# Converted weights of a hybrid decoder step held as half-unit tiles instead of whole-unit tiles

## The chip, the cores and the metric

The kernel runs on one core of a Trainium2 chip. The metric is the device time of one execution in microseconds (us); the time of a kernel is the median of several runs. A measurement is compared with runs of the kernel before on the same chip.

## The reference

The reference is one inference step of a decoder trunk with two layers, for a prompt of 512 tokens and eight samples of four new tokens, 544 columns in all, with 1024 features:

```
h = x
layer 0:  h += SSD(rmsnorm(h))     # in: 1024 -> 5120 + 32, convolution of width 4, scan, gate, norm, out: 2048 -> 1024
          h += MLP(rmsnorm(h))     # square(relu(u @ w_up)) @ w_down, 1024 -> 4096 -> 1024
layer 1:  h += HGRN2(rmsnorm(h))   # in: 1024 -> 4 x 1024, recurrence, gate, norm, out: 1024 -> 1024
          h += MLP(rmsnorm(h))
y = rmsnorm(h)
```

It returns y for both parts and the new states of convolution, SSD and HGRN2. Everything is float32.

## The kernel before, in words

**Products of two parts.** A float32 matrix is not multiplied as it is. Each weight and each operand is split into a high part (a cast to float32r, `hi`) and a low part (`lo = raw - hi`), and a product is the sum of three: hi times high, hi times low, lo times high. `split` (L187) does it with one cast on ScalarE (L188) and one subtraction on VectorE (L189).

**Units.** Weights arrive as units of 128 x 1024 float32, half a megabyte: eight blocks of 128 x 128. For an input or MLP unit the blocks are the eight k of one output tile; for an output unit (`out_unit`, and the end of `hgrn`) they are four k times two output tiles, so that block `k * 256 + i * 128` belongs to k and output tile i, and both halves of the unit hold two k of both tiles. There are 56 units of the SSD layer, 64 of each MLP and 40 of HGRN2.

**From DRAM to TensorE.** `load_next` (L166) loads a unit into one of three raw tiles over SyncE's queue; a load waits until the raw tile it overwrites has been read for the last time. `conv_unit` (L191) issues the loads that are due and then converts one unit: a cast into a tile `whi` and a subtraction into a tile `wlo`, each 128 x 1024, each tag with two buffers (pool `wcv`, L104). So a cast waits until the last matmul that read `whi` of the unit two back is done, and a subtraction likewise for `wlo`. The first two units are converted in two pieces of 512 columns into the same tiles. In the SSD layer every third unit from 6 on is "added" (L221): its low part is made ahead by `added_low` (L224), a negated cast on ScalarE into a tile of its own and two accumulating DMAs from GpSimd's queue, so that `conv_unit` has only the cast left (L206). `take` (L252) is called when a unit is needed and converts up to one unit ahead.

**TensorE's order.** `products` (L298) issues, for one unit and one output tile, three products per k in two column halves of 272: 48 matmuls for eight k. In the SSD layer (`"w" in sp`) they go in groups of four k: first hi with both operand parts for the four, then lo. Elsewhere k by k. The results stand in `acc`, two PSUM tiles of two banks each (`psb`).

**The MLP** computes a quarter of its columns directly and the rest by a scheme of seven products on 2 x 2 blocks (`seventh`, `form`); these take tiles `fh` and `fl` of 128 x 512 with five buffers of their own. In the last three quarters the first two down units are cut (L79): d0 k 0 to 3, the last products of the scheme, d0 k 4 and 5, d1 k 0 to 5, d0 k 6 and 7, d1 k 6 and 7, then the other units. The last two down units of the kernel go to `finish` (L1362), which multiplies and norms column half by column half.

**What sets the order of work.** The program is traced in Python. Beside the units, generators run as background: `scan`, `gated_norm`, `levels`, `states` and others give up control with a number of ticks, and `products` ticks after every six pairs of matmuls. The framework then orders each engine's instructions by priority and by a model of when they are ready, hands out buffers, and sets semaphores. Loads (L196) and, outside the MLPs, conversions (L201) have high priority from unit 3 on. On the chip each engine works through its own list in order, and an instruction that has to wait holds up those behind it. SyncE's list holds weight loads (L171), the decay rows of the scan read back from DRAM (`rows`, L558, tile `w`), states (L620, L741) and the convolution's output (L470).

In the SSD layer, ScalarE and VectorE do, beside the conversions: `conv_tile` (L466 to L483: copies `pre` out of PSUM, the convolution `cacc`, `th`, then `xs` or `BC`), the decay weights (L568 to L571 `E` and `w`, L623), the scan (`xd`, `xt`, `hT`, `y`), the gates (L505 `thz`, L506 `zs`) and the gated norm (L763 on; its split of `yh` and `yl` at L772 and after).

Of the kernel before, what the change touches and what calls it, by code (L numbers as in the profile page):

```python
# [16 lines left out]
P = 128  # L17
# [79 lines left out]
def trunk(ctx: ExitStack, tc: tile.TileContext, io):  # L97
# [93 lines left out]
    def conv_unit():  # L191
        if state["conv"] >= len(jobs):
            return
        (kind, u), at = jobs[state["conv"]]
        state["conv"] += 1
        with tc.high_priority() if u > 2 else ExitStack():  # L196
            while state["load"] <= min(at + (3 if mp else 2 if "w" in sp else 1), len(loads) - 1):
                if loads[state["load"]][0] != "u" and not mp:
                    break
                load_next()  # L200
        with tc.high_priority() if u > 2 and not mp else ExitStack():  # L201
            if kind == "u":
# [12 lines left out]
            else:  # L215
                hi, lo = form(kind, u)
        ready[kind, u] = (hi, lo)

    lows = {}

    def added(u):  # L221
        return 3 < u < U_MLP and u % 3 == 0

    def added_low(u):  # L224

        raw = loaded["u", u]
        lows[u] = sp["w"].tile([P, 1024], F32R, tag="wlo", bufs=1, name=f"wlo{u}")
        nc.scalar.activation(lows[u], raw, AF.Copy, scale=-1.0)
        for c in (0, 512):
            nc.gpsimd.dma_start(lows[u][:, c : c + 512], io["W"][u][:, c : c + 512], accum_op=ADD)  # L230

    def form(name, u):

        a1 = loaded["u", u]
        v = loaded.get(("v", u))
        if name == "n6":
            s2 = mp["w"].tile([P, 512], F32, tag="s2", bufs=2, name=f"s2_{u}")
            nc.vector.tensor_tensor(s2, v[:, :512], a1[:, :512], ADD)
# [11 lines left out]
        return hi, lo  # L250

    def take(key):  # L252
        i = place[key]
# [11 lines left out]
    def unit(u):  # L265
        return take(("u", u))
# [28 lines left out]
            while any(e[2] == name for e in q):  # L295
                step(q)

    def products(ps, hi, lo, ops, first, last):  # L298

        n = len(ops)  # L300
        order = [(k, j) for k in range(n) for j in range(3)]
        if "w" in sp:

            order = [(k, j) for k0 in range(0, n, 4) for js in ((0, 1), (2,)) for k in range(k0, min(k0 + 4, n)) for j in js]
        for i, (k, j) in enumerate(order):
            oh, ol = ops[k]
            w, o = ((hi, oh), (hi, ol), (lo, oh))[j]
            for h in range(2):
                nc.tensor.matmul(  # L309
                    ps[:, h, :HF], w[:, k, :], o[:, h * HF : (h + 1) * HF],  # L310
                    start=(first and i == 0), stop=(last and i == len(order) - 1),
                )
            if i % 6 == 5:
                tick()
# [88 lines left out]
    def ssd(then):  # L403
# [51 lines left out]

        def conv_tile(u, ct, dst, rep):

            hi, lo = unit(u)
            ps = acc_tile(f"ps{u}")
            products(  # L460
                ps, hi.rearrange("p (k m) -> p k m", m=P), lo.rearrange("p (k m) -> p k m", m=P), uops, True, True
            )
# [31 lines left out]
            return pool.tile([P, T], F32, tag="zs", bufs=4, name=f"zs{u}")  # L494

        def z_product(u, ops=uops):
            hi, lo = unit(u)
            ps = acc_tile(f"ps{u}")
            products(ps, hi.rearrange("p (k m) -> p k m", m=P), lo.rearrange("p (k m) -> p k m", m=P), ops, True, True)
            return ps  # L500

        def silu2(u, zs, z):
# [5 lines left out]
        def first_gates():  # L508

            nonlocal rb  # L510
            zs = [zs_tile(u) for u in range(4)]
            w = [[t.rearrange("p (k m) -> p k m", m=P) for t in unit(u)] for u in range(2)]
            ps = [acc_tile(f"ps{u}") for u in range(2)]
            for k in range(KT):
                for i in range(2):
                    products(ps[i], w[i][0][:, k : k + 1], w[i][1][:, k : k + 1], xops[k : k + 1], k == 0, k == KT - 1)
            for i in range(2):
                nc.scalar.copy(v3(zs[i]), ps[i][:, :, :HF])
            res = []
# [399 lines left out]
    def mlp(name, plan, v0, then, last=False):  # L919
# [47 lines left out]
                yield 2.6  # L967

        background(operands(), name, wait=3)
        m8 = lambda w: w.rearrange("p (k m) -> p k m", m=P)  # L970

        def up(u):
            ps = acc_tile(f"pm{u}")
            products(ps, *map(m8, unit(u)), uops, True, True)
            return ps

        def g_tiles(u, a):
# [14 lines left out]
        def seventh(name_, u):  # L992
# [8 lines left out]
            hi, lo = map(m8, take((name_, u)))  # L1001
            for k in range(4):
                oh, ol = fops[name_, k]
                for j, (w, o) in enumerate(((hi, oh), (hi, ol), (lo, oh))):
                    nc.tensor.matmul(  # L1005
                        ps, w[:, k, :], o, start=(name_ in ("p1", "p2", "q7") and k == 0 and j == 0),
                        stop=(k == 3 and j == 2), skip_group_check=name_ in ("n6", "n5", "p3", "q4"),
                    )
            tick()
# [26 lines left out]
        for x_ in plan:  # L1036
# [9 lines left out]
            elif x_[0] == "d":  # L1046
                _, u, k0, k1, m, q = x_
                if k0 == 0:
# [4 lines left out]
                    if last and q == MLP_GROUPS - 1 and m >= KT - 2:  # L1053
# [6 lines left out]
                    acc[m][1] = [m8(w) for w in unit(u)]  # L1060
                ps, (hi, lo) = acc[m]
# [12 lines left out]
    def hgrn(then):  # L1074
# [37 lines left out]
        background(rstd_steps(1.0 / D, "hn", res, nt, wait=3), "hn", wait=3)  # L1112

        def product(u):
            hi, lo = unit(u)
            ps = acc_tile(f"ps{u}")
            products(ps, hi.rearrange("p (k m) -> p k m", m=P), lo.rearrange("p (k m) -> p k m", m=P), uops, True, True)
            return ps

        def project(u, name, ps=None):  # L1120
# [224 lines left out]
        for half in range(2):  # L1345
            if half:
                drain("hs7")
            for mp in range(4):
                hi, lo = unit(u)
                u += 1  # L1350
                for i in range(2):
                    ps = acc_tile(f"pho{half}_{mp}_{i}")
                    products(
                        ps, hi.rearrange("p (k m) -> p k m", k=4)[:, :, i * P : (i + 1) * P],
                        lo.rearrange("p (k m) -> p k m", k=4)[:, :, i * P : (i + 1) * P], ops[4 * half : 4 * half + 4], True, True,
                    )
                    add_to_x(2 * mp + i, ps, then if half == 1 else None)
        es.close()

# [2 lines left out]
    def finish(w, ops, pss):  # L1362

        es = ExitStack()
        pool = es.enter_context(tc.tile_pool(name="f_pool", bufs=2, reuse_waits="tile"))
        ws = [[t.rearrange("p (k m) -> p k m", m=P) for t in hl] for hl in w]
        ms2 = (KT - 2, KT - 1)
        for h in range(2):
            hs = slice(h * HF, (h + 1) * HF)
            sqs = []  # L1370
            for m, (hi, lo), ps in zip(ms2, ws, pss):
                for k, (oh, ol) in enumerate(ops):
                    for j, (a, o) in enumerate(((hi, oh), (hi, ol), (lo, oh))):
                        nc.tensor.matmul(
                            ps[:, h, :HF], a[:, k, :], o[:, hs], start=(k == 0 and j == 0), stop=(k == len(ops) - 1 and j == 2)
                        )
                sq = pool.tile([P, HF], F32, tag=f"sq{m}", name=f"sq{m}_{h}")
                nc.vector.tensor_tensor(x[m][:, hs], ps[:, h, :HF], x[m][:, hs], ADD)
# [171 lines left out]
```

## Time and profile before

| | |
|---|---|
| time before, median of 3 runs | 1575.24 us (1573.57 to 1576.04) |
| the profiled execution: its own time | 1573.53 us |
| the profiled execution: its span | 1571.7 us |
| mean granted clock of TensorE | 0.991 |
| casts of whole or half units, L188 / L206 | 161 / 17 |
| subtractions of units, L189 | 161 |

The span runs from the first to the last instruction that the profile shows; the time around it is 1.8 us in that execution. In the profile PE is TensorE's matmuls, PEld its weight loads, DVE VectorE, ACT ScalarE, POOL GpSimd, SP SyncE; a q behind the name means the engine's sequencer. A row names line, engine, operation, and output <- inputs by the program's names without buffer numbers; L188 and L189 are lines of a helper, so that only the tile's name tells whose conversion it is. Starts are in us from the span's start. A tile's low part made by `added_low` is also called `wlo`.

### The profile page before, as it was taken

What the parts mean: (1) busy time and instruction counts of PE and PEld (TensorE: products, weight loads), DVE (VectorE), ACT (ScalarE), POOL (GpSimd) and SP (SyncE); (2) the same over time, 40 slices, a digit from 0 to 9 for tenths busy, and PEclk for the clock granted to TensorE, in tenths of its full rate; (3) what the DMA queues carried; (4) which work ended last, traced back from release to release, by engine and by line L of the source; (5) the groups of instructions that cost most, each with busy time, mean ns of one, the idle gap of its engine ahead of it and who ended that gap; (6) DMA issues with size and microseconds to landing.
All of it is one profiled execution on the core that took longest, in us unless ns stands there. A gap on an engine that the chain in (4) does not pass through costs nothing.

```text
span 1571.7 us, 32262 instructions
## 1 busy us (share of the span) xinstructions
PE 1539.2 (98%) x13420; PEld 1477.0 (94%) x13420; DVE 1081.3 (69%) x1985; ACT 741.6 (47%) x1332; POOL 122.4 (8%) x195
## 2 busy tenths in 40 slices
PE   8999899999999999999999999999999999999997
PEld 7998789898999999999999999999999999999996
DVE  7878698968877555474655788888877655474544
ACT  5666675665344436273553332333344446263552
POOL 3112011110001001010000000000001001010001
PEclk9999899999999999999999999999999999999998
DMA  6545547574436245463323232323226245463311
GB/s 197 154 129 138 150 107 227 121 220 123 129 103 181 86 121 135 121 166 81 116 63 108 69 99 84 105 89 110 70 96 175 81 128 128 121 166 93 105 55 57
DMA packets 86337, 188.90 MB, mean 120 GB/s; under 512 B 12784, under 2 KB 33168, under 8 KB 86192
## 3 DMA queue, kind: packets, MB, share of 16 engines
q1 hardware_dynamic: 73120, 164.21, 33.3%
q0 software_dynamic: 11808, 21.50, 8.5%
q8 instruction: 105, 1.72, 0.5%
q10 hardware_dynamic: 1264, 1.14, 0.2%
q14 instruction: 40, 0.33, 0.1%
HBM read 169.64 MB, written 17.18 MB: 119 GB/s over the span
## 4 chain that ended last, share of the span: by engine, by line
PE 90%; DVE 3%; ACT 3%; DMA 2%; issue 1%; POOL 0%; POOLq 0%; SPq 0%; ACTq 0%; DVEq 0%
PE ps L309 25%; PE pd L309 23%; PE pp L1005 11%; PE pm L309 6%; PE po L309 6%; PE pc L1005 5%; PE pho L309 3%; DMA w<-cum_d 1%; DVE wlo L189 1%; PE pa L1144 1%; ACT whi L188 1%; PE py L602 1%; ACT w L570 1%; PE pS L1247 1%; PE po L1270 1%
## 5 line engine op out<-in xcount | busy, mean ns | idle before, releaser
L188 ACT CAST whi<-raw 128x1024 fp32r<-128x1024 f32 (+1 forms) x161 | 167.1, 1038 | 337.6 <-PE ps L309 110.5
L189 DVE TENSOR_TENSOR wlo<-raw,whi 128x1024 fp32r<-128x1024 f32 (+1 forms) x161 | 195.6, 1215 | 35.3 <-ACT whi L188 30.1
L309 PE MATMUL pd<-gh,wlo 128*128 128x272 f32 x992 | 205.8, 289 | 0.8
L309 PE MATMUL pd<-gh,whi 128*128 128x272 f32 x992 | 205.8, 288 | 0.0
L309 PE MATMUL pd<-gl,whi 128*128 128x272 f32 x992 | 205.3, 288 | 0.0
L309 PEld LDWEIGHTS pd<-gh,wlo 128*128 128x128 f32 x992 | 155.6, 188 | 2.1 <-DVE wlo L189 2.1
L309 PEld LDWEIGHTS pd<-gh,whi 128*128 128x128 f32 x992 | 156.0, 188 | 0.0
L309 PEld LDWEIGHTS pd<-gl,whi 128*128 128x128 f32 x992 | 155.5, 188 | 0.0
L309 PE MATMUL ps<-uh_s,whi 128*128 128x272 f32 x576 | 125.0, 298 | 8.1 <-DVE zs L506 6.7
L398 DVE TENSOR_TENSOR x<-pd,x 128x544 f32<-128x544 f32 x62 | 44.7, 722 | 122.7 <-PE pd L309 122.7
L309 PE MATMUL ps<-ul_s,whi 128*128 128x272 f32 x576 | 121.1, 291 | 0.0
L309 PE MATMUL ps<-uh,whi 128*128 128x272 f32 x512 | 112.1, 300 | 0.0
L309 PE MATMUL ps<-uh,wlo 128*128 128x272 f32 x512 | 106.9, 289 | 0.0
L309 PE MATMUL ps<-ul,whi 128*128 128x272 f32 x512 | 106.4, 289 | 0.0
L309 PEld LDWEIGHTS ps<-uh_s,whi 128*128 128x128 f32 x576 | 91.4, 191 | 14.6 <-issue 13.0
L309 PEld LDWEIGHTS ps<-ul_s,whi 128*128 128x128 f32 x576 | 91.7, 191 | 0.1
L181 POOL DMA_DIRECT2D v<-in_W x48 | 42.1, 1030 | 601.2 <-DMA v<-in_W 407.3
L309 PE MATMUL ps<-uh_s,wlo 128*128 128x272 f32 x576 | 85.6, 291 | 0.0
L309 PEld LDWEIGHTS ps<-uh,whi 128*128 128x128 f32 x512 | 80.5, 189 | 3.7 <-issue 1.4
L309 PEld LDWEIGHTS ps<-uh,wlo 128*128 128x128 f32 x512 | 80.4, 188 | 0.0
L309 PEld LDWEIGHTS ps<-ul,whi 128*128 128x128 f32 x512 | 80.3, 189 | 0.0
L309 PEld LDWEIGHTS ps<-uh_s,wlo 128*128 128x128 f32 x576 | 78.2, 191 | 0.0
(428 smaller groups left out, 3803.8 us busy)
## 6 DMA issues: line engine op xcount, KB each, us to landing
raw<-in_W SPq DMA_DIRECT2D x198, 512.0 KB, 3.6
v<-in_W SPq DMA_DIRECT2D x48, 256.0 KB, 4.3
v<-in_W POOLq DMA_DIRECT2D x48, 256.0 KB, 5.7
wlo<-in_W POOLq DMA_DIRECT2D x34, 256.0 KB, 6.6
st<-in_ssm_in SPq DMA_DIRECT2D x16, 512.0 KB, 6.3
w<-cum_d SPq DMA_DIRECT2D x16, 512.0 KB, 5.6
out_ssm_s<-st SPq DMA_DIRECT2D x16, 512.0 KB, 6.2
a<-in_W SPq DMA_DIRECT2D x24, 256.0 KB, 4.2
```

The source lines that it names most:

```text
L181: nc.gpsimd.dma_start(raw[:, c : c + 512], io["W"][u + 1][:, :512], accum_op=ADD)
L188: nc.scalar.copy(hi, raw)
L189: (eng or nc.vector).tensor_tensor(lo, raw, hi.bitcast(F32), SUB)
L309: nc.tensor.matmul(ps[:, h, :HF], w[:, k, :], o[:, h * HF : (h + 1) * HF], start=(first and i == 0), stop=(last and i == len(order) - 1),)
L398: nc.vector.tensor_tensor(v3(x[m]), ps[:, :, :HF], v3(x[m]), ADD)
L570: nc.scalar.activation(w[:, h], w[:, h], AF.Relu, bias=tok[:, 1, c, 8 * g + h : 8 * g + h + 1], scale=-1.0)
L602: nc.tensor.matmul(py[64 * (h % 2) : 64 * (h % 2) + 64, (h // 2) * P : (h // 2 + 1) * P], xds[c][:, h], ws_[c][:, h], start=True, stop=True,)
L1005: nc.tensor.matmul(ps, w[:, k, :], o, start=(name_ in ("p1", "p2", "q7") and k == 0 and j == 0), stop=(k == 3 and j == 2), skip_group_chec ...
L1144: nc.tensor.matmul(pv4[b * NS : (b + 1) * NS, c], K[:, bs], QQ[:, 2 - n :, bs], start=True, stop=True, tile_position=(0, b * NS),)
L1247: nc.tensor.matmul(pS[:, c * P : (c + 1) * P], kt[:, c], vt[:, c], start=True, stop=True)
L1270: nc.tensor.matmul(po[:, cs], att[:, c], vt[:, c], start=True, stop=(c == 0))
```

## The change

The pool of converted weights gets four buffers per tag instead of two, and a tile is half as large, 128 x 512; the memory is the same. `conv_unit` allocates two halves of each part and converts the unit half by half: cast, subtraction, cast, subtraction (for an "added" unit two casts). `ready` holds lists of tiles, and `block` finds a block's tile and column. The low part made by `added_low` stays one tile of 1024 with one negated cast; only two slices of it are handed on. `form` puts its single tiles into lists of one. `products` takes the pair of lists, the first column and the step from k to k; its order of matmuls, their shapes and number stay as they were, as do loads, raw tiles, the tick and all other pools.

```diff
-    wcv = ctx.enter_context(tc.tile_pool(name="wcv", bufs=2))
+    wcv = ctx.enter_context(tc.tile_pool(name="wcv", bufs=4))
...
                 raw = loaded.pop(("u", u))
-                hi = wcv.tile([P, 1024], F32R, tag="whi", name=f"whi{u}")
-                if added(u):
-                    nc.scalar.copy(hi, raw)
-                    lo = lows.pop(u)
-                else:
-                    lo = wcv.tile([P, 1024], F32R, tag="wlo", name=f"wlo{u}")
-                    for a in (0, 512) if u < 2 else (None,):
-                        c = slice(None) if a is None else slice(a, a + 512)
-                        split(raw[:, c], hi[:, c], lo[:, c])
+                hi = halves("whi", u)
+                lo = lows.pop(u) if added(u) else halves("wlo", u)
+                for a in range(2):
+                    c = raw[:, 512 * a : 512 * a + 512]
+                    if added(u):
+                        nc.scalar.copy(hi[a], c)
+                    else:
+                        split(c, hi[a], lo[a])
                 if added(u + 1):
                     added_low(u + 1)
...
+    def halves(tag, u):
+        return [wcv.tile([P, 512], F32R, tag=tag, name=f"{tag}{u}_{a}") for a in range(2)]
...
-        lows[u] = sp["w"].tile([P, 1024], F32R, tag="wlo", bufs=1, name=f"wlo{u}")
-        nc.scalar.activation(lows[u], raw, AF.Copy, scale=-1.0)
-        for c in (0, 512):
-            nc.gpsimd.dma_start(lows[u][:, c : c + 512], io["W"][u][:, c : c + 512], accum_op=ADD)
+        lo = sp["w"].tile([P, 1024], F32R, tag="wlo", bufs=1, name=f"wlo{u}")
+        nc.scalar.activation(lo, raw, AF.Copy, scale=-1.0)
+        lows[u] = [lo[:, :512], lo[:, 512:]]
+        for a in range(2):
+            nc.gpsimd.dma_start(lows[u][a], io["W"][u][:, 512 * a : 512 * a + 512], accum_op=ADD)
...
+    def block(w, c):
+
+        return w[c // 512][:, c % 512 : c % 512 + P]
+
-    def products(ps, hi, lo, ops, first, last):
+    def products(ps, w, ops, first, last, c0=0, step=P):
...
-            w, o = ((hi, oh), (hi, ol), (lo, oh))[j]
+            a, o = ((w[0], oh), (w[0], ol), (w[1], oh))[j]
             for h in range(2):
                 nc.tensor.matmul(
-                    ps[:, h, :HF], w[:, k, :], o[:, h * HF : (h + 1) * HF],
+                    ps[:, h, :HF], block(a, c0 + k * step), o[:, h * HF : (h + 1) * HF],
...
-            w = [t.rearrange("p (k m) -> p k m", k=4) for t in unit(u)]
+            w = unit(u)
             for i in range(2):
                 ps = acc_tile(f"po{g}_{j}_{i}")
-                products(ps, *(t[:, :, i * P : (i + 1) * P] for t in w), ops[g], True, True)
+                products(ps, w, ops[g], True, True, i * P, 2 * P)
...
-                products(ps, hi[:, k0:k1], lo[:, k0:k1], [g[gb + k] for k in range(k0, k1)], k0 == 0, k1 == 8)
+                products(ps, w, [g[gb + k] for k in range(k0, k1)], k0 == 0, k1 == 8, k0 * P)
```

The other callers (`conv_tile`, `z_product`, `first_gates`, `up`, `seventh`, `product`, the end of `hgrn`, `finish`) change in the same way.

More of the change, by code (lines that the diff above doesn't have):

```diff
@@ L249, in form @@
         split(raw, hi, lo)
-        return hi, lo
+        return [hi], [lo]
     def take(key):
@@ L456, in conv_tile @@
         def conv_tile(u, ct, dst, rep):
-            hi, lo = unit(u)
+            w = unit(u)
             ps = acc_tile(f"ps{u}")
-            products(
-                ps, hi.rearrange("p (k m) -> p k m", m=P), lo.rearrange("p (k m) -> p k m", m=P), uops, True, True
-            )
+            products(ps, w, uops, True, True)
             pre = p2.tile([P, 571], F32, tag="pre", name=f"pre{ct}")
@@ L496, in z_product @@
         def z_product(u, ops=uops):
-            hi, lo = unit(u)
+            w = unit(u)
             ps = acc_tile(f"ps{u}")
-            products(ps, hi.rearrange("p (k m) -> p k m", m=P), lo.rearrange("p (k m) -> p k m", m=P), ops, True, True)
+            products(ps, w, ops, True, True)
             return ps
@@ L511, in first_gates @@
             zs = [zs_tile(u) for u in range(4)]
-            w = [[t.rearrange("p (k m) -> p k m", m=P) for t in unit(u)] for u in range(2)]
+            w = [unit(u) for u in range(2)]
             ps = [acc_tile(f"ps{u}") for u in range(2)]
@@ L969, in mlp @@
         background(operands(), name, wait=3)
-        m8 = lambda w: w.rearrange("p (k m) -> p k m", m=P)
         def up(u):
+            w = unit(u)
             ps = acc_tile(f"pm{u}")
-            products(ps, *map(m8, unit(u)), uops, True, True)
+            products(ps, w, uops, True, True)
             return ps
@@ L1000, in seventh @@
             ps = d[{"p2": "b", "q7": "c", "q4": "c"}.get(name_, "a")]
-            hi, lo = map(m8, take((name_, u)))
+            hi, lo = take((name_, u))
             for k in range(4):
@@ L1005, in seventh @@
                     nc.tensor.matmul(
-                        ps, w[:, k, :], o, start=(name_ in ("p1", "p2", "q7") and k == 0 and j == 0),
+                        ps, block(w, k * P), o, start=(name_ in ("p1", "p2", "q7") and k == 0 and j == 0),
                         stop=(k == 3 and j == 2), skip_group_check=name_ in ("n6", "n5", "p3", "q4"),
@@ L1059, in mlp @@
                         continue
-                    acc[m][1] = [m8(w) for w in unit(u)]
-                ps, (hi, lo) = acc[m]
+                    acc[m][1] = unit(u)
+                ps, w = acc[m]
                 gb = u - 8 - m
-                products(ps, hi[:, k0:k1], lo[:, k0:k1], [g[gb + k] for k in range(k0, k1)], k0 == 0, k1 == 8)
+                products(ps, w, [g[gb + k] for k in range(k0, k1)], k0 == 0, k1 == 8, k0 * P)
                 if k1 == 8:
@@ L1114, in product @@
         def product(u):
-            hi, lo = unit(u)
+            w = unit(u)
             ps = acc_tile(f"ps{u}")
-            products(ps, hi.rearrange("p (k m) -> p k m", m=P), lo.rearrange("p (k m) -> p k m", m=P), uops, True, True)
+            products(ps, w, uops, True, True)
             return ps
@@ L1348, in hgrn @@
             for mp in range(4):
-                hi, lo = unit(u)
+                w = unit(u)
                 u += 1
@@ L1352, in hgrn @@
                     ps = acc_tile(f"pho{half}_{mp}_{i}")
[L1353 to L1356, printed above, removed]
+                    products(ps, w, ops[4 * half : 4 * half + 4], True, True, i * P, 2 * P)
                     add_to_x(2 * mp + i, ps, then if half == 1 else None)
@@ L1370, in finish @@
             sqs = []
-            for m, (hi, lo), ps in zip(ms2, ws, pss):
+            for m, (hi, lo), ps in zip(ms2, w, pss):
                 for k, (oh, ol) in enumerate(ops):
@@ L1374, in finish @@
                         nc.tensor.matmul(
-                            ps[:, h, :HF], a[:, k, :], o[:, hs], start=(k == 0 and j == 0), stop=(k == len(ops) - 1 and j == 2)
+                            ps[:, h, :HF], block(a, k * P), o[:, hs], start=(k == 0 and j == 0), stop=(k == len(ops) - 1 and j == 2)
                         )
```

4 lines of the change are left out of this document (2 added, 2 removed).

## The prediction

> **What bounds the kernel now.** The page's first and fourth parts come first.
>
> ```profile
> PE 1539.2 (98%) x13420; PEld 1477.0 (94%) x13420; DVE 1081.3 (69%) x1985; ACT 741.6 (47%) x1332; POOL 122.4 (8%) x195
> PE 90%; DVE 3%; ACT 3%; DMA 2%; issue 1%; POOL 0%; POOLq 0%; SPq 0%; ACTq 0%; DVEq 0%
> PE ps L309 25%; PE pd L309 23%; PE pp L1005 11%; PE pm L309 6%; PE po L309 6%; PE pc L1005 5%; PE pho L309 3%; DMA w<-cum_d 1%; DVE wlo L189 1%; PE pa L1144 1%; ACT whi L188 1%; PE py L602 1%; ACT w L570 1%; PE pS L1247 1%; PE po L1270 1%
> ```
>
> TensorE (PE) is busy 98% of the span and is 90% of the chain that ended last. A change that touches only the conversion of weights, on ScalarE (ACT) and VectorE (DVE), can win no more than the time in which TensorE waits. The view of busy time by stage (columns: PE, PEld, DVE, ACT, POOL, granted clock, DMA) says where that is.
>
> ```profile
> 40.00:200.00 160.00, 148.53 (x1141) 139.00 (x1142) 125.44 (x210) 100.03 (x201) 22.31 (x48) 0.95 0.52 143
> 200.00:480.00 280.00, 277.18 (x2234) 258.64 (x2234) 228.15 (x370) 161.90 (x306) 32.24 (x53) 1.00 0.55 150
> 480.00:1440.00 960.00, 958.87 (x8859) 932.04 (x8858) 628.84 (x1237) 403.50 (x696) 46.62 (x66) 1.00 0.39 110
> ```
>
> From 480 to 1440 us TensorE idles 1.1 of 960 us; there is nearly nothing to win, and ACT (42%) and DVE (66%) have room. Between 40 and 480 it idles 14.3 us, and between 40 and 200 its clock averages 0.95. The view of waits says what it waits for; the last row is ACT's.
>
> ```profile
> PEld pd L309 <- DVE wlo L189: 2.1, 6, 0.4
> PEld ps L309 <- ACT whi L188: 0.3, 1, 0.3
> PE ps L309 <- DVE zs L506: 6.7, 1, 6.7
> ACT whi L188 <- PE ps L309: 110.5, 39, 7.3
> ```
>
> Weights themselves are late only six times, 2.1 us in all. The other way round there is more: ACT stands 39 times ahead of a cast, 110.5 us, until TensorE has let go of the buffer two units back. That costs only where something urgent is queued behind the cast.
>
> **The change part by part.** *More instructions.* These rows (minimum, median, maximum in ns) give the price of a whole and of a half.
>
> ```profile
> L188 ACT CAST whi<-raw x161: 606/1049/1057, 4.1 to 1543.3; 128x1024 fp32r<-128x1024 f32 x157, 128x512 fp32r<-128x512 f32 x4
> L188 ACT CAST fh_p<-raw x48: 613/620/624, 554.2 to 1488.7; 128x512 fp32r<-128x512 f32 x48
> L189 DVE TENSOR_TENSOR wlo<-raw,whi x161: 677/1220/1576, 4.7 to 1544.4; 128x1024 fp32r<-128x1024 f32 x157, 128x512 fp32r<-128x512 f32 x4
> L189 DVE TENSOR_TENSOR fl_p<-raw,fh_p x48: 681/691/695, 554.8 to 1489.4; 128x512 fp32r<-128x512 f32 x48
> ```
>
> Successive instructions overlap: below, the cast at 157.33 lasts 1.05 us and the next starts 0.96 after it, and the subtraction at 158.42 lasts 1.23 and the next starts 1.14 after it, 0.09 each. So a whole cast occupies ACT 0.96, two halves 2 x 0.53 = 1.06, 0.10 more; on DVE 2 x 0.60 = 1.20 against 1.13, 0.07 more. 174 casts (157 and the 17 of "added" units) make 17 us of ACT, 157 subtractions 11 us of DVE. In the stage 480 to 1440 TensorE's own work covers both. In the first 480 us DVE is busy 80%; 56 casts and 39 subtractions there make 5.6 + 2.7 = 8.3 us, which is the price if no cover is left. I put 0.2 us on the path, since conversions are some 2% of the chain (wlo 1%, whi 1% in the page); below nothing is excluded, because these are added instructions.
>
> *More waits on TensorE.* A unit now has four first readers instead of two. Satisfied waits cost nothing here: the stage of 960 us has some 100 units with two each and idles 1.1 us. An unsatisfied one is the rivals' matter. Loads and their queue (SP) keep their number; a raw tile is freed by the last half subtraction.
>
> *Late weights in the MLP.* Chain of waits, the hand-over after the split down units:
>
> ```profile
> 620.82 5.79 PE pd L309 x46
> 626.63 1.06 ACT whi L188
> 627.71 1.24 DVE wlo L189
> 628.99 11.08 PE pd L309 x86
> ```
>
> The cast waits until the unit two back is done, then cast and subtraction run one after the other, and TensorE arrives first. Once halves are tiles, the half for k 0 to 3 is free since the first piece of that unit, several us before, and only k 4 to 7 is converted after 626.6, needed 3 us into the next unit. All six waits go: -2.1 us. What would be late next, the second half, has 2 us to spare.
>
> *Gap B, 158.3 to 164.95.* ACT's, DVE's and TensorE's timelines (start, length; idle before in brackets):
>
> ```profile
> 157.33 1.05 ACT L188 CAST whi<-raw 128x1024 fp32r<-128x1024 f32 x1 [6.96 <-PE ps L309]
> 158.29 0.67 ACT L479 ACTIVATE th<-cacc 128x568 f32<-128x568 f32 x1
> 154.50 0.79 DVE L476 SCALAR_TENSOR_TENSOR cacc<-pre,vh,cacc 128x568 f32<-128x568 f32 x1
> 158.42 1.23 DVE L189 TENSOR_TENSOR wlo<-raw,whi 128x1024 fp32r<-128x1024 f32 x1 [1.92 <-ACT whi L188]
> 159.56 0.68 DVE L480 SCALAR_TENSOR_TENSOR BC<-th,cacc 128x512 f32<-128x512 f32 x1
> 164.95 0.79 PE L309 MATMUL ps<-uh_s,whi 128*128 128x272 f32 x2 [6.65 <-DVE zs L506]
> ```
>
> th had its input at 155.29 but stood behind the cast; DVE idled 1.92 us, subtracted, and went on to the work that TensorE's bank waits for. With halves the first is converted in the idle time (its buffer is free after k 3), and at 157.33 only a half cast is left: 157.33 + 0.62 + 0.60 = 158.55 against 159.56, so the gap is 1.0 us shorter.
>
> *Gap A, to 128.27.* The chain and TensorE's row:
>
> ```profile
> 98.74 1.23 DVE wlo L189
> 100.37 6.29 DMA w<-cum_d
> 109.66 1.24 DVE wlo L189
> 111.29 8.55 DMA w<-cum_d
> 128.27 1.55 PE L602 MATMUL py<-w,xd 128*64 128x128 f32 x12 [3.29 <-DVE xts L687]
> ```
>
> SP issues the raw load once the subtraction has freed its tile, and the decay rows (w) only behind it. A cast and subtraction in series take about 0.95 + 1.24 = 2.2; halves overlap, 0.53 + 0.62 + 0.69 = 1.84, 0.4 less at 109.66; at 98.74 between nothing and 0.54, I take 0.3. The gap shrinks by 0.7.
>
> Both gaps are followed by half clock (PE busy is the column behind the length):
>
> ```profile
> 124.20:127.60 3.40, 0.78 (x2) 0.00 (x0) 2.79 (x6) 3.19 (x8) 0.27 (x1) 1.00 0.19 29
> 127.60:134.40 6.80, 6.13 (x36) 4.77 (x40) 6.66 (x13) 5.25 (x13) 0.58 (x3) 0.50 0.47 147
> 161.70:172.00 10.30, 7.05 (x31) 6.91 (x32) 7.07 (x20) 4.90 (x8) 0.00 (x0) 0.50 0.67 218
> ```
>
> If TensorE resumes earlier inside a stretch at 0.50 that ends at the same time, half of it is won: I book -0.5 for B; for A, part of whose gain is at full clock, -0.5. [...]
>
> *Gap D, 447.5 to 450.08.*
>
> ```profile
> 446.58 1.05 ACT L188 CAST whi<-raw 128x1024 fp32r<-128x1024 f32 x1 [4.61 <-issue]
> 447.53 0.64 ACT L188 CAST yh<-zs 128x544 fp32r<-128x544 f32 x1
> 448.22 0.77 PE L309 MATMUL po<-yh,whi 128*128 128x272 f32 x4 [0.72 <-ACT yh L188]
> 450.08 0.52 PE L309 MATMUL po<-yl,whi 128*128 128x272 f32 x2 [1.09 <-DVE yl L189]
> ```
>
> The same pattern: yh behind a cast. Output units read both halves in both products, so both come free late; still only a half cast stands ahead of yh (-0.4) and a half subtraction ahead of yl (-0.5). Of 1.81 us I take -0.6.
>
> Sum: 0.2 - 2.1 - 0.5 - 0.5 - 0.6 = -3.5 us. The profiled execution took 1573.53, so 1570.0; its median stands 1.7 higher at 1575.24, and the forecast there is **1571.7 us**.
>
> **Rivals.** *R1, the clock or the order falls well.* A keeps full clock: 6.8 us at 0.50 hold 3.4 us of full work, of which 0.3 is already booked, so -3.1: 1568.6. If also th is put between the two half casts at B, it runs at 155.3, and BC right behind DVE's work that ends at 156.5 instead of at 159.56: another 2 us beyond the 1.0, at half clock and up, 1 to 2: about 1567. For it: the 6.96 us of idle ACT. Against it: the order is fixed when the program is built, and nothing shows it.
>
> *R2, gains and shifts cancel.* The 2.1 us of the MLP come, but the first 480 us, where ACT, DVE and SP interlock, lose about what I booked: 1575.24 - 2.1 + 1 = 1574.
>
> *R3, a second wait at the head of ACT's queue: slower.* The first half cast is free to stand earlier in ACT's order. If TensorE is then later than that order assumed, ACT stands at the first half and what used to run before the cast (th, the Exp of w, the copies pre that empty TensorE's banks) stands behind it. Price: the mean wait of the row above, 110.5/39 = 2.8 us, for each urgent place, and with it one more 3.4 us stretch at half clock, 1.7. It decides once the wait for the first half outlasts the urgent work's own input. At two of A, B and D, and with the MLP's gain: 2 x 4.5 - 2.1 = +6.9, 1582. For it: gaps B and D already have this form. Against it: the half buffer comes free two thirds of a unit earlier than the whole. [...] If 8.3 us of added instructions all lay on the path, 1575.24 + 8.3 - 2.1 = 1581.4 would come out too.
>
> **How the numbers follow.** Chances: forecast 0.35, R1 0.12, R2 0.27, R3 0.26. The range leaves out the far end of R1 and the upper half of R3: 1566 to 1581. The likeliest case alone spans 1569 to 1573. A measurement of this kernel can tell about 0.2%, 3.2 us, from no change; the forecast of -0.22% lies just past that. Faster by more: 0.45 (R1 and most of the forecast); within: 0.29; slower by more: 0.26.
>
> **What would show it.** In the new profile the row of PEld pd waiting for wlo is gone, which settles the MLP; whi casts are near 0.62 us and wlo near 0.69; gaps A, B and D are near 2.6, 5.7 and 1.2 us. R1 shows as a clock above 0.95 in 40 to 200; R3 as larger gaps there, with th, E or yh behind a cast that waits for PE. The forecast is wrong if the stage 480 to 1440 idles more than now, or if the order of ACT's work in the first 480 us comes out otherwise.

## The result and the profile after

The changed kernel takes 1576.76 us (median of 18 runs, 1574.66 to 1582.21), the kernel before 1575.26 on the same chip (18 runs, 1572.07 to 1576.54). The ratio, taken over all runs and not from the two medians, is 1.0018, 95% interval 1.0012 to 1.0025: 2 to 4 us slower, where 3.5 us faster was forecast. The profiled execution took 1580.26 us, 6.7 more than that of before, so it lies at the slow end of its runs, and what it shows is larger than the mean loss.

The page's first and fourth parts of the changed kernel:

```profile
PE 1542.1 (98%) x13420; PEld 1479.3 (94%) x13420; DVE 1093.9 (69%) x2142; ACT 769.6 (49%) x1506; POOL 121.9 (8%) x195
PE 74%; DVE 1%; DMA 1%; issue 1%; ACT 1%; POOL 0%; POOLq 0%; ACTq 0%; DVEq 0%; SPq 0%
```

The 157 subtractions and 174 casts more are there (DVE x2142, ACT x1506). TensorE has as many matmuls as before, but at 513 of the 13420 places of its list another product stands: the framework ordered that list anew as well. The same stages as before:

```profile
40.00:200.00 160.00, 146.78 (x1145) 136.67 (x1138) 125.89 (x220) 103.15 (x221) 23.94 (x48) 0.96 0.53 142
200.00:480.00 280.00, 274.06 (x2188) 254.17 (x2187) 227.78 (x385) 163.00 (x335) 26.94 (x50) 0.99 0.54 146
480.00:1440.00 960.00, 959.45 (x8867) 933.01 (x8867) 638.17 (x1351) 423.63 (x808) 49.38 (x70) 1.00 0.39 111
```

From 480 us on TensorE idles less than before (0.55 us for 1.13). Ahead of that it idles 1.75 us more from 40 to 200 and 3.1 more from 200 to 480. Two rows of the tiles' view, of before and of after, fix the place: the first product of the first MLP (pm) is TensorE's entry into the late stage (minimum, median, maximum in ns, then first and last start).

```profile
L309 PE MATMUL pm<-uh,whi x256: 283/287/373, 473.8 to 1229.4; 128*128 128x272 f32 x128
```

```profile
L316 PE MATMUL pm<-uh,whi x256: 283/287/373, 481.6 to 1237.0; 128*128 128x272 f32 x128
```

The first layer ends 7.8 us later; everything after it is 1.1 us shorter (6.7 at the end). Idle time up to there is 4.6 us more (19.4 in before, 24.0 here). The clock takes another 1.7: six stretches of 3.41 us at half clock instead of five. The two behind gap A are gone, but there is one more behind gap B, and two are new (at 11.5 and at 393.8). The last 1.5 us is not taken apart. So two questions: what happened in the first 480 us, and why did the later layers not give 2.1.

For the second, the waits. The row of PEld pd waiting for wlo is gone, as forecast; but another one has grown, here in before and after:

```profile
PEld pp L1005 <- ACT s L1014: 2.9, 12, 0.3
```

```profile
PEld pp L1009 <- ACT s L1018: 4.3, 18, 0.3
```

Such a row is idle time of the weight loads, which overlap the matmuls (in the changed kernel 1479.3 us of loads and 1542.1 of matmuls lie in a span of 1578.4), so it is not TensorE's loss. That comes out of the starts of TensorE's matmuls, compared one by one with those of before: 2.4 us is won at the six late weights, and some 0.8 us is lost again at the products of the up-projection (pp and pc), which also stand in another order.

**Gap B** got longer, not shorter. ACT, DVE and TensorE of the changed kernel:

```profile
155.53 0.62 ACT L188 CAST whi<-raw 128x512 fp32r<-128x512 f32 x1 [4.68 <-PE ps L316]
156.06 0.67 ACT L484 ACTIVATE th<-cacc 128x568 f32<-128x568 f32 x1
159.80 1.28 ACT L573 ACTIVATE E<-w 64x512 f32<-64x512 f32 x2 [3.07 <-DMA w<-cum_d]
161.10 1.57 ACT L575 ACTIVATE w<-w,tok 128x128 f32<-128x128 f32 x5
162.58 0.64 ACT L373 ACTIVATE ssq<-y 128x544 f32<-128x544 f32 x1
163.97 0.60 ACT L510 ACTIVATE thz<-ps 128x544 f32<-128x544 f32 x1
164.73 0.71 DVE L511 SCALAR_TENSOR_TENSOR zs<-thz,ps 128x544 f32<-128x544 f32 x1
165.59 0.79 PE L316 MATMUL ps<-uh_s,whi 128*128 128x272 f32 x2 [9.10 <-DVE zs L511]
```

What was forecast did happen: only a half cast stands ahead of th, and th runs at 156.06 instead of 158.29. But behind it the list is another one. In the kernel before, ACT goes on with the squares of the gated norm (ssq) and thz, and comes to the E and w of the next scan last:

```profile
161.67 0.66 ACT L366 ACTIVATE ssq<-y 128x544 f32<-128x544 f32 x1 [2.71 <-DVE y L763]
162.87 0.60 ACT L505 ACTIVATE thz<-ps 128x544 f32<-128x544 f32 x1
170.76 1.28 ACT L568 ACTIVATE E<-w 64x512 f32<-64x512 f32 x2 [4.42 <-DMA w<-cum_d]
```

In the changed kernel E and w stand first and wait 3.07 us for the DMA of the decay rows; ssq and thz wait behind them, and TensorE with them.

**A new gap at 390.** DVE and TensorE:

```profile
386.22 0.68 DVE L611 TENSOR_TENSOR y<-py,y 128x512 f32<-128x512 f32 x1
389.83 0.41 DVE L711 TENSOR_TENSOR ws<-ws,tok 32x256 f32<-32x256 f32 x1 [2.93 <-DMA ws<-cum_d]
390.17 1.21 DVE L628 TENSOR_TENSOR w<-w,cb 128x1024 f32<-128x1024 f32 x1
392.72 1.09 PE L607 MATMUL py<-w,xd 128*64 128x128 f32 x16 [2.53 <-DVE xts L692]
```

The small product ws, which waits for a DMA, stands ahead of w, for which TensorE waits; in the kernel before, w runs at 382.73 and ws behind it at 385.62. The clock of TensorE, in stretches of 3.41 us, shows what comes on top: half speed (0.51) for the stretch that follows.

```profile
390.47:393.87 3.40, 1.15 (x17) 1.01 (x18) 3.34 (x7) 1.26 (x4) 0.00 (x0) 1.00 0.02 5
393.88:397.29 3.41, 3.41 (x16) 2.78 (x20) 3.33 (x7) 3.11 (x9) 0.00 (x0) 0.51 0.12 19
```

2.5 idle and 1.7 lost to the clock make 4.2 us in this execution. **Theory:** the halves are sound; the framework draws up each engine's list by a schedule of its own, from the lengths and the readiness of all instructions, and with 331 instructions more, and shorter ones, it drew up another list in which urgent work stands behind a DMA wait (*order*). **Rivals:** the added instructions lie on the path (*added work*); a half cast that waits at the head of ACT's queue holds up what is behind it (*second wait*, R3).

### The profile page after: what moved, and what is told of

It reads as the page before. It is cut to its first block, busy times and chain, and to the rows that moved or that the text cites. A ratio compares the mean times of both kernels' runs of the same rounds, so it can differ in the third digit from the quotient of the medians.

```text
span 1578.4 us, 32682 instructions
## 1 busy us (share of the span) xinstructions
PE 1542.1 (98%) x13420; PEld 1479.3 (94%) x13420; DVE 1093.9 (69%) x2142; ACT 769.6 (49%) x1506; POOL 121.9 (8%) x195
## 4 chain that ended last, share of the span: by engine, by line
PE 74%; DVE 1%; DMA 1%; issue 1%; ACT 1%; POOL 0%; POOLq 0%; ACTq 0%; DVEq 0%; SPq 0%
PE pd L316 24%; PE ps L316 16%; PE pp L1009 11%; PE pm L316 6%; PE pc L1009 5%; PE pho L316 3%; PE po L316 3%; PE pa L1148 1%; PE po L1274 1%; PE pS L1251 1%; PE pa L1167 0%; PE pd L1374 0%; PE po L1276 0%; DMA ws<-cum_d 0%; DMA w<-cum_d 0%
## 5 line engine op out<-in xcount | busy, mean ns | idle before, releaser
L188 ACT CAST whi<-raw 128x512 fp32r<-128x512 f32 x318 | 195.1, 618 | 407.3 <-PE ps L316 160.5
L189 DVE TENSOR_TENSOR wlo<-raw,whi 128x512 fp32r<-128x512 f32 x318 | 219.6, 693 | 101.7 <-ACT whi L188 99.6
```

Of the source, the lines that this page charges most:

```text
L189: (eng or nc.vector).tensor_tensor(lo, raw, hi.bitcast(F32), SUB)
```

## The experiments

Most of them hold the order of an engine's instructions, with edges between neighbours (NoSync) that are there for the order alone. They stand at the end of the recorded program:

```diff
+    for e, text in PINNED.items():
...
+                    tc.add_manual_dep(
+                        i, last.name, mybir.DependencyInfo(mybir.DependencyClass.NoSync, mybir.DependencyReason.DATA),
...
```

PINNED is a list of places, by engine; the conversions (whi and wlo of units) have a numbering of their own, so that they can be left out of it or not.

**x1 and x2, halves and order exchanged.** x1 is the changed kernel with all else in the order of before, x2 the kernel before with all else in the order of the changed one; conversions are left out of the list and placed freely.

> The changed kernel, with every instruction that is no weight conversion held in the order that it has in the kernel before, on all five engines; only the half conversions are placed freely, and they land nearly where they land in the changed kernel. Order theory (the halves are sound, but with other lengths to place the list of ACT's and DVE's work in the first 480 us came out differently, urgent work behind a DMA wait): faster than before, 1571 to 1574 us, no 2.5 us idle before TensorE's w,xd work at 390, gap B under 6.7 us. Added-work theory (174 casts and 157 subtractions more lie on the path in the first 480 us): slower by 2 to 5, 1577 to 1580. Second-wait theory (a half cast stands at the head of ACT's queue ahead of urgent work): 1577 to 1582, since the halves stand where they stand in the changed kernel.

> The counterpart: the kernel before, whole conversions and whole tiles, with every other instruction held in the order that it has in the changed kernel. Order theory: slower than before by 3 to 8 us, 1578 to 1583, with the 2.5 us idle at 390 and a gap B near 9 us. Added-work theory and second-wait theory: nothing was added, so within 1.5 us of before, 1574 to 1577.

x1: 1574.46 us, ratio to before 0.9998 (0.9989 to 1.0007). x2: 1599.97, ratio 1.0169 (1.0147 to 1.0191). With the old order the loss is gone, though every half is there. And the order does more than was expected of it: a list drawn up around halves costs wholes some 26 us, with a gap B of 11.4 us. But x1 didn't win what order theory promised either. Its first layer ends at 473.6, level with before; gap B is 5.68 us as forecast and gap A, with the half clock behind it, is gone, yet all is given back by 480. In the MLP a new wait replaces the late weights. Rows of x1; the first stands at 2.9 us and 12 times in the kernel before, the second, TensorE's own idle time, does not occur there:

```profile
PEld pp L1012 <- ACT s L1021: 7.2, 18, 0.8
PE pp L1012 <- ACT s L1021: 3.0, 6, 0.6
```

DVE, ACT and TensorE of x1 show where from:

```profile
590.07 0.68 DVE L189 TENSOR_TENSOR wlo<-raw,whi 128x512 fp32r<-128x512 f32 x1
590.68 0.68 DVE L244 TENSOR_TENSOR s<-v,raw 128x512 f32<-128x512 f32 x1
591.28 0.43 DVE L1029 TENSOR_TENSOR a_n<-pc,sv 128x272 f32<-128x272 f32 x1
591.75 0.66 ACT L1037 ACTIVATE a_n<-a_n 128x544 f32<-128x544 f32 x1 [0.84 <-DVE a_n L1029]
594.19 0.39 ACT L1021 COPY s<-pp 128x272 f32<-128x272 f32 x1
594.63 0.39 PE L1012 MATMUL pp<-m_b2h,fh_p 128*128 128x272 f32 x1 [0.49 <-ACT s L1021]
```

The same place of the kernel before:

```profile
590.07 0.69 DVE L238 TENSOR_TENSOR s<-v,raw 128x512 f32<-128x512 f32 x1
590.68 0.43 DVE L1022 TENSOR_TENSOR a_n<-pc,sv 128x272 f32<-128x272 f32 x1
```

A first half is free to run sooner than the whole was; its subtraction went ahead of work for which TensorE waits, one step of DVE (0.60 us) each time. That is the *early-half* theory, and x5 tests it. It happens in the first layer too: at 224 two half subtractions (219.46 and 222.15) stand ahead of the y for which TensorE waits; x5, below, has both behind it. TensorE in x1 and in x5:

```profile
224.19 0.47 PE L747 MATMUL pn<-xq,bm 128*128 128x512 f32 x1 [1.95 <-DVE y L614]
221.13 0.47 PE L747 MATMUL pn<-xq,bm 128*128 128x512 f32 x1 [0.74 <-DVE y L614]
```

Not every place of the first layer was followed up in this way.

**x3 and x4, halves in some layers only.** Two fixed slots of a whole unit instead of the pool, and the conversion in halves from the first MLP on (x3) or only ahead of it (x4):

```diff
-    wcv = ctx.enter_context(tc.tile_pool(name="wcv", bufs=4))
+    wcv = ctx.enter_context(tc.tile_pool(name="wcv", bufs=1))
+    cv = [wcv.tile([P, 2, 1024], F32R, name=n) for n in ("whi", "wlo")]
```

> Two fixed slots of a whole unit for each part; whole conversions in the first (state space) layer, halves from the first MLP on. The order in the first layer is that of the kernel before. Order theory: as before up to 480 us, then 0.5 to 1 us won per MLP, 1573 to 1575. The prediction's term for the MLPs alone: -2.1, 1573.1. Added-work theory: about 118 units with 0.17 us more each are mostly covered there, at most +1: 1574 to 1576. Second-wait theory: no change here, 1574 to 1575.

> The same slots, halves in the first layer only and whole conversions from the first MLP on. Order theory: all the loss and none of the MLP's gain, 1577 to 1581, with the order of the changed kernel in the first layer. Added-work theory: 1577 to 1580 too, so the two runs before this tell these apart. Second-wait theory: 1578 to 1583. If the loss is in the later layers: 1572 to 1575.

1586.58 us (ratio 1.0071, 1.0059 to 1.0084) and 1587.48 (1.0080, 1.0066 to 1.0094): outside of what any theory said, and alike whichever part is halved. Both compute something else, it seems because some products read the weights of another unit (this was not traced), so that these are not the times of this computation, and nothing follows from them. x10 and x11 ask the question again.

**x5, halves side by side.** The complete order of before, conversions included, each whole replaced by its two halves next to each other. Against x1 only the places of half casts and half subtractions differ.

> Half tiles, and the complete order of the kernel before, with every whole conversion replaced by its two halves side by side at its place (x1 left the halves free, and its first halves stood earlier: in each group of the split up-projection a half subtraction of 0.60 us ahead of the difference that ends in the copy of s, for which TensorE then waited 0.5 to 0.6 us more). Early-half theory (what the half tiles win is taken back by first halves that stand earlier on DVE than the whole did): gains of the MLPs, of gaps A, B and D stay, 3 to 5 us faster than before, no larger wait of PEld pp for s than before. Added-work theory (the 157 extra subtractions and 174 extra casts themselves take the gain back): as x1, within 1.5 us of before. Order theory alone (halves bring nothing, only the order counts): within 1 us of before.

1567.12 us (1566.25 to 1567.76), ratio 0.9958 (0.9946 to 0.9970): 6.6 us faster than before, with 331 instructions more. Added work is out, and early-half theory holds in the time; TensorE's own wait for s, 3.0 us in x1, has no row any more. But the row of PEld is not back at the 2.9 us of before, as was expected, so that row does not measure the loss. Its rows: waits and stages, then the end of the first layer.

```profile
PEld pp L1012 <- ACT s L1021: 4.1, 18, 0.3
```

```profile
480.00:1440.00 960.00, 959.75 (x8882) 934.48 (x8881) 631.99 (x1339) 417.63 (x806) 45.92 (x66) 1.00 0.38 110
```

```profile
L319 PE MATMUL pm<-uh,whi x256: 283/287/373, 469.8 to 1224.0; 128*128 128x272 f32 x128
```

The first layer ends 4.0 us sooner than in before, and the late stage idles 0.25 us.

**x6, x7, x8, the changed kernel with single moves.** Its own complete order, but for ws put behind w at 390 (x6: one instruction of DVE), ssq, gsq and thz put ahead of E and w at gap B (x7: six instructions of ACT go ahead, and two of w go behind two half casts that followed them), and both (x8). All else keeps its place.

> The changed kernel in its own complete order, with one move on DVE: the product that waits for the DMA of ws (at 389.83 in its profile) goes from ahead of w to its place in the kernel before, five instructions later. Order theory: the 2.5 us idle at 390 and the stretch of half clock behind it go, 2 to 4 us faster than the changed kernel, 1572.5 to 1575. If that gap is only what one execution had, 0 to 1 us faster, 1576. Theories that put the loss on the halves themselves: no change against the changed kernel, 1577.

> The changed kernel in its own complete order, with one stretch of ACT's list put back as in the kernel before: the squares of the gated norm and thz ahead of the Exp of the next scan's decay rows, which wait for a DMA. Order theory: gap B shrinks from 9.1 to between 5.7 and 7 us, part of it at half clock, 1 to 3 us faster than the changed kernel, 1574 to 1576. Theories that put the loss on the halves: no change, 1577.

> Both moves of the two runs before this. Order theory: their gains add, 3 to 6 us faster than the changed kernel, 1571 to 1574, level with or under the kernel before. Otherwise 1576 to 1577.

x6: 1574.18, ratio to before 1.0006 (0.9997 to 1.0016). x7: 1572.42, 0.9992 (0.9983 to 1.0001). x8: 1571.00, 0.9978 (0.9969 to 0.9987). Against the changed kernel's 1.0018 the moves win 1.9, 4.1 and 6.3 us (each the difference of the ratios times 1574): their gains add, as far as intervals of almost 2 us to each side can tell, and the changed kernel with both moves is faster than before. x6 won less than the 4.2 us seen in one execution and a little less than was expected of it, x7 more. In x8 the idle at 390 is gone and gap B is 6.88 us:

```profile
160.59 0.79 PE L319 MATMUL ps<-uh_s,whi 128*128 128x272 f32 x2 [6.88 <-DVE zs L514]
```

**x9, pieces on whole tiles.** The kernel before with every unit converted in two pieces, in the order of x5 instruction by instruction. Only the release differs: a half buffer comes free with its whole.

```diff
-                    for a in (0, 512) if u < 2 else (None,):
-                        c = slice(None) if a is None else slice(a, a + 512)
-                        split(raw[:, c], hi[:, c], lo[:, c])
+                for a in (0, 512):
+                    c = slice(a, a + 512)
...
```

> The same order as x5, instruction by instruction, and the same half casts and half subtractions, but on whole tiles, two of each part as in the kernel before: a half buffer comes free only with its whole. If x5's 6.6 us come from the early release of halves: none of the gain, 1574 to 1579 (before, plus what 174 casts and 157 subtractions cost when nothing covers them). If they come from cast and subtraction overlapping by halves: 1567 to 1570. Half and half: about 1571.

1568.07 us, ratio 0.9959 (0.9947 to 0.9972), against 0.9958 of x5. The gain is that of the pieces: cast and subtraction overlap, and TensorE can begin on the first piece (both with their times in the MLP below). The runs do not part these two. The early release, which is what half tiles are for, adds nothing that the times show, with intervals of 2 us to each side; between the two profiled executions it is 1.1 us (the last norm's first product, fn_pc, starts at 1542.1 and 1543.2). Where it can be seen is gap B, with both casts behind the wait and th behind them:

```profile
154.23 1.14 ACT L188 CAST whi<-raw 128x512 fp32r<-128x512 f32 x2 [6.86 <-PE ps L311]
155.28 0.67 ACT L481 ACTIVATE th<-cacc 128x568 f32<-128x568 f32 x1
161.48 0.79 PE L311 MATMUL ps<-uh_s,whi 128*128 128x272 f32 x2 [6.29 <-DVE zs L508]
```

6.29 us against 5.69 in x5. In the MLP the pieces do without it. DVE and TensorE of x9 at the place where the weights were late:

```profile
624.22 1.28 DVE L189 TENSOR_TENSOR wlo<-raw,whi 128x512 fp32r<-128x512 f32 x2
625.40 0.41 PE L311 MATMUL pd<-gh,wlo 128*128 128x272 f32 x2
```

From the start of the cast (623.33) to the end of the second subtraction are 2.17 us, hardly less than the 2.31 of before, but TensorE takes the low part at 625.40 without a wait, 0.1 us ahead of that end: the first piece is enough.

**x10 and x11, side by side in one part.** x10 holds the halves side by side in the first layer and leaves them free after it, x11 the other way round; all else is in the order of before.

> As x5 in the first layer (halves side by side), as x1 from the first MLP on (halves placed freely). Early-half theory, by the offsets of x1 and x5: -4 from the first layer and +1 from the rest, 1570 to 1571. If only the later layers matter: 1574. If only the first matters: 1567.

> The counterpart: halves placed freely in the first layer, side by side from the first MLP on. Early-half theory: 0 to -0.5 from the first layer and -3 from the rest, 1570.5 to 1571.5. If only the first layer matters: 1574; if only the later layers: 1567.

1571.26 us, ratio 0.9983 (0.9974 to 0.9992), and 1570.50, ratio 0.9980 (0.9969 to 0.9991). The two parts win 2.7 and 3.1 us and add to 5.8 of x5's 6.6: within the intervals, early halves cost about as much in the first layer as after it.

**x12, pieces in free order.** x9 without the list: the same instructions and the same tiles, in the order that the framework draws up.

> The pieces on whole tiles of x9 with no order prescribed: the kernel before, in which every unit (not only the first two) is converted in two pieces. A first piece can't stand earlier than the whole's buffer comes free, but the list is drawn up anew from the other lengths. If only early first halves spoil the order: 1567 to 1570, near x9. If any new list is a throw of the dice: anything between 1568 and 1580; above 1572 says that the order which happened to come out costs what the pieces win.

1577.45 us, ratio 1.0017 (1.0005 to 1.0028). The same work takes 9 us less in another order (0.9959 against 1.0017). Here no first half comes free ahead of its whole, and there is no idle of TensorE for s as in x1, so early halves aren't needed for a loss: another new list brought one. This one has an E ahead of gsq and thz at gap B again; at 261 the norm's small products (nwr) stand behind BC, which waits for th, which stands behind an E that waited 4.6 us for its DMA; and all of yh stands behind the negated cast of an added unit at 451.9:

```profile
163.57 0.80 PE L308 MATMUL ps<-uh_s,whi 128*128 128x272 f32 x2 [8.65 <-DVE zs L505]
263.18 2.22 PE L352 MATMUL gn_pr<-ident,nwr 128*128 128x128 f32 x10 [2.10 <-DVE nwr L336]
453.54 0.77 PE L308 MATMUL po<-yh,whi 128*128 128x272 f32 x4 [1.76 <-ACT yh L188]
```

## Why the prediction was wrong, step by step

**The step that failed** is none of the sum's terms but what stands under all of them: each edit was priced at its place in the order of before, "the order is fixed when the program is built, and nothing shows it", as it says against R1. It isn't a given of the kernel: it is drawn up from the same instructions that the change replaces, so a new order is a cost of the change, and the sum put it at nothing. The prediction named this as what would make it wrong; it gave the good side of it a price (R1), and of the bad side only one form (R3, a half cast that waits for TensorE). x8 shows 6.3 us for nine instructions moved, x9 against x12 9 us for the order alone. In the order that the sum assumed (x5) the change wins 6.6 us, more than the 3.5 of the sum. That x8, with an order of its own, comes out at 3.5 too is chance: it wins 3.0 by the end of the first layer and 1.3 after it, not the terms of the sum.

**More instructions, 0.2 us.** Right where they stand in the place of the whole: x5 and x9 carry all of them and are the fastest two. Wrong where a first half stands earlier: x1 gives back 6.3 us against x5 (ratios 0.9998 and 0.9958). Between the two profiled executions it is 8.1 us: 3.8 in the first layer (473.6 against 469.8), where only the place at 224 has been followed up, and 4.3 after it, of which 3.0 are TensorE's waits for s, behind half subtractions of 0.60 us. The cover was not missing in sum, DVE has time (in x1 it is busy for 637.0 of the 960 us from 480 to 1440); it was missing at the place.

**Late weights in the MLP, -2.1 us.** The six waits went, in every kernel with halves or pieces (x3 and x4 aside). In x5 the rest of the program after the first layer is 3.3 us shorter (first pm at 469.8, against 473.8 in before, and fn_pc at 1542.1 against 1549.4): 2.4 us at the six places, as booked, and 1.0 at the pp products, which the sum left out. The reason was wrong: the half that comes free early isn't needed, since x9 has none and wins 2.9 there; that TensorE can begin on the first piece is enough. In the changed kernel as it was built, pp and pc took some 0.8 us back.

**Gap B, -1.0 us, -0.5 booked.** As forecast in the order of before: 6.65 to 5.68 in x1 and 5.69 in x5; 0.6 of it is the early half cast (x9: 6.29). TensorE kept nearly all of it in x5, since the half clock behind it lasted as long as before (10.24 us) and moved with the gap. In the changed kernel it became 9.10, by the order.

**Gap A, -0.7 and -0.5 booked.** Too little, and in part for a reason that the sum does not have. In x5 the gap shrank from 3.29 to 0.69 us:

```profile
124.60 1.09 PE L610 MATMUL py<-w,xd 128*64 128x128 f32 x16 [0.69 <-DVE xts L695]
w<-cum_d SPq DMA_DIRECT2D x1, 512.0 KB, 6.4
```

The decay rows are issued 1.5 us sooner (109.78 instead of 111.29); the overlap of half casts and half subtractions gives some of it, since the two take 1.92 us there instead of 2.28, as forecast. The second row is their DMA: it lands after 6.4 us, where it took 8.55 in before, which the sum took as given. With halves or pieces it is 6.3 to 6.9 us in every profiled execution (x3 and x4 aside), but 6.4 in x2 too, which has whole conversions; so this isn't shown to be the halves' doing, and the cause stays open. The half clock behind the gap went in all profiled executions with halves or pieces but that of x7 (x3 and x4 aside). This part of R1 is what happened, in part by luck, since the gap shrank by more than the sum gives. Of its -3.1 not all stayed: TensorE then waits 1.5 us at 135 and 0.3 at 140, and at 140 x5 is 2.5 us better off for gap A.

**Gap D, -0.6.** In x5 both waits are there still, 0.31 for yh and 1.32 for yl, together 0.2 less than the 1.81 of before: smaller than booked; in TensorE's starts nothing is left of it.

**R3** had the right form and price, a waiting instruction ahead of urgent work and a stretch of half clock behind it, 4.5 us a place; at 390 it was 4.2 in the profiled execution, though moving ws (x6) won 1.9. But what waits is not a half cast for TensorE, it is E and ws for a DMA, and no wait was added to any of them. Its premise, a first half that stands earlier, did come true, but it cost on DVE (x1 against x5). The forecast of 1581.4 if all 8.3 us of added work lay on the path is refuted by x5.

What stays open: why the 18 runs of the changed kernel spread over 7.5 us and the five of x5 over 1.5. Part of it is the clock: its mean is 0.993 in all five runs of x5, 0.989 to 0.992 in those of the changed kernel and 0.989 to 0.993 (mean 0.9916) in the 29 of before that were measured beside x5. By these means (0.0014 of some 1570 us), some 2 of x5's 6.6 us are half clock that it does not meet, an estimate. Only one execution of each kernel has been profiled, so what brings it on in one run and not in another is not known. Nor was x2's larger loss taken apart.

## What to carry to other kernels

Where a scheduler orders the engines' queues, a change of lengths or of tiles is two changes, the one meant and a new order; price the second, and separate them by holding the order of the kernel before, which here turned a loss of 0.2% into a gain of 0.4%. Work that may start earlier is not free: in x1 a half subtraction that stood earlier held up what DVE had to do next by 0.60 us, so hold such work at the place where it is needed. And ask which part of an idea does the work: here the shorter pieces did nearly all of it, and the half tiles little or nothing.

## What the runs showed of the hardware

Up to the last norm, the stretches at half clock last 6.83 and 10.24 us in the profile of before, and 3.41, 13.65 and 3.41 us in that of after: one to four times 3.41 us. The stretches at full clock between them are whole multiples of it too (27.31 us in before; 146.77 and 218.45 in after, which are 8, 43 and 64 times 3.413). With both profiles laid out in cells of 3.41 us from these borders, these are all the cells at full clock that hold less than 2.5 us of TensorE's work:

| profile | cell from (us) | TensorE busy (us of 3.41) | clock of the next cell |
|---|---|---|---|
| before | 158.34 | 0.00 | 0.50 |
| after | 158.32 | 0.00 | 0.50 |
| before | 124.21 | 0.77 | 0.50 |
| after | 390.43 | 1.12 | 0.50 |
| after | 154.91 | 1.59 | 1.00 |
| before | 14.98 | 1.89 | 1.00 |
| after | 8.13 | 1.92 | 0.50 |
| before | 38.88 | 1.96 | 1.00 |
| after | 4.72 | 2.19 | 1.00 |
| after | 127.60 | 2.23 | 1.00 |
| before | 448.48 | 2.32 | 1.00 |
| before | 4.74 | 2.36 | 1.00 |
| after | 96.88 | 2.37 | 1.00 |
| after | 100.29 | 2.43 | 1.00 |

No busier cell of the two was followed by half clock. The length of a gap does not order the cases in this way. x8 has a gap of 1.82 us from 126.45, with 2.45 and 2.55 us of work in the two stretches that it touches, and the clock stays:

```profile
124.00:127.41 3.41, 2.45 (x26) 2.06 (x22) 3.29 (x6) 0.21 (x2) 0.00 (x0) 1.00 0.40 98
127.42:130.83 3.41, 2.55 (x21) 1.20 (x22) 3.38 (x8) 3.41 (x11) 0.54 (x3) 1.00 0.20 55
130.83:134.24 3.41, 3.41 (x28) 3.32 (x27) 3.41 (x7) 3.41 (x11) 0.92 (x1) 1.00 0.56 163
```

x12's shorter gap of 1.76 us lies in one stretch, with 1.65 us of work, and the next is at half clock:

```profile
451.22:454.63 3.41, 1.65 (x11) 1.22 (x10) 3.04 (x5) 3.41 (x7) 1.39 (x2) 0.98 0.11 12
454.64:458.05 3.41, 3.41 (x17) 3.41 (x17) 1.51 (x3) 0.49 (x1) 0.35 (x1) 0.52 0.94 204
```

So a gap of about 1.8 us cost 1.7 us more (half of 3.41, an estimate) in one of these two executions, and nothing in the other.
